# Columns 2 to 5 of an output projection by seven half-size products a pair instead of eight

## The chip, the cores and the metric

One core of one Trainium2 chip runs one launch of one decoder layer over 512 tokens of width 1024. The metric is the device time of the launch in microseconds, the median of several runs.

## The reference, cut to what matters

```python
h = x + 0.5 * swiglu(rmsnorm(x, g1), w1_in, w1_out)            # first feed-forward
h = h + hybrid_mixer(rmsnorm(h, gm), ...)                      # the mixer
h = h + 0.5 * swiglu(rmsnorm(h, g2), w2_in, w2_out)            # second feed-forward
y = rmsnorm(h, final)

def hybrid_mixer(u, ...):
    ...
    y = sigmoid(gate_h) * y_h + sigmoid(gate_g) * y_g          # (512, 1024), two merged branches
    return y @ w_out                                           # (1024, 1024): the output projection
```

The change is in the last line, `y @ w_out`, and in the adding of its result to `h`.

## The kernel before, in words

Activations lie transposed: a tile of 128 partitions (channels) by 512 tokens for each of eight channel blocks. A product in fp32 accuracy is three matmuls of float32r operands: both factors are split into a high part (a cast on ACT) and a low part (a subtraction on DVE), and `mm3` (lines 199 to 202) adds high x high, high x low and low x high in PSUM.

The layer has three stages: the first feed-forward, the mixer, the second feed-forward. Within the feed-forwards, and in nearly all of the mixer, the order of the work is fixed by hand or by a planner (`Desk`, which plays engines and tile rings in Python and issues instructions in that order). The mixer's output projection (lines 2250 to 2254) stands outside of both: there the framework's own scheduler orders the instructions, by priority and by its own estimate of durations, and moves them in front of one another.

What matters here, in the order of the program:

- `merged(d)` (line 1900) makes operand d of the output projection: it loads the branch and gate tiles (SP), combines them on DVE (lines 1917, 1920, 1923), and splits the result into `ms[d]`, high part by ACT (line 1930) and low part by DVE (line 1932). The eighth one comes last, after the last branch product.
- The output projection is a loop over eight output columns d. For each, SP loads the residual `hd[d]`, which the first feed-forward had spilled, and the two halves of the weight column (line 193, 256 KB each, into a ring `raw` of RB = 3 tiles); `slab` splits each half (ACT cast, line 195; DVE subtraction, line 196) into a ring `wp` of WB = 6 pairs (two tags of three); `dense` runs 8 x 3 matmuls of 512 columns; DVE adds half of the PSUM to the residual (line 2254) into `h[:, d]`.
- `nextnorm` (line 692) then prepares the second feed-forward for column d: `uh`, `ul` (ACT line 226, DVE line 227), a square (ACT, line 236), and its addition to `acc` on POOL (line 238). For d = 7 the addition is on DVE (line 697).
- The second feed-forward begins with plain units of four blocks each (12 matmuls of 512 columns). Its weights first come through the same `raw` and `wp` rings (line 311; casts on line 344, subtractions on line 319). After the first unit, PE runs the statistics matmul `pst` (line 247), which reads `acc`; matmuls behind it wait for it, since an engine runs its instructions in order. The loads into the feed-forward's own ring `rw` wait until the mixer's memory is free, which is after line 697.
- The feed-forwards already use seven products for eight in their large parts (`seven`, `fast`): there, an operand's low part is now and then made by an ACT negation (line 348) and an accumulating transfer on POOL that adds the weight from DRAM (line 349).

## Time and profile before

| | |
|---|---|
| device time, median of 3 runs | 1548.21 us (1547.71 to 1548.64) |
| the profiled execution's own time | 1547.87 us |
| its span in the trace | 1546.1 us |
| PE busy | 1535.9 us, 99% |
| DVE / ACT / POOL busy | 1179.7 / 887.9 / 409.0 us |
| granted TensorE clock, mean | 0.999 |

The profiled execution took 1.8 us beyond its span and 0.34 us less than the median. A busy PE means that matmuls are in its pipeline; how fast they follow one another is read from the distance of their starts. All times below are microseconds from the start of the span.

### The profile page before, as it was taken

The numbers are of one execution on the slowest core, as the hardware profiler recorded it, in microseconds if no ns is written. First come the engines' busy times: TensorE is split into PE (matmuls) and PEld (weight loads), VectorE is DVE, ScalarE is ACT, GpSimd is POOL, SyncE is SP. The second block draws the span as 40 slices with busy tenths as digits, with TensorE's granted clock in tenths as the row PEclk, the third lists the DMA queues.
The fourth block names the chain that finished last, engine by engine and source line by source line (L and its number), as shares of the span: only waits on it lengthen the run. The fifth ranks groups of instructions, "written<-read, shape, count | busy, mean of one in ns | idle before, by whom it ended". The sixth has DMA issues, their size and how long they took to land.

```text
span 1546.1 us, 29433 instructions
## 1 busy us (share of the span) xinstructions
PE 1535.9 (99%) x10660; PEld 1340.0 (87%) x10660; DVE 1179.7 (76%) x2257; ACT 887.9 (57%) x1965; POOL 409.0 (26%) x727
## 2 busy tenths in 40 slices
PE   9999999999999999999999999999999999999998
PEld 8899998988888888888888878888888899999897
DVE  6988887678786778678888887865554799988765
ACT  5766776454454345556676676555423576676543
POOL 0211221110221212536534655450001221121000
PEclk9999999999999999999999999999999999999999
DMA  5866866543213223654463675566554587786751
GB/s 190 190 167 171 190 163 150 154 120 109 84 45 94 65 81 117 191 181 147 134 208 119 190 224 164 171 191 187 153 192 130 157 185 194 194 194 172 192 123 64
DMA packets 159538, 237.57 MB, mean 154 GB/s; under 512 B 23312, under 2 KB 54672, under 8 KB 159392
## 3 DMA queue, kind: packets, MB, share of 16 engines
q1 hardware_dynamic: 138944, 199.63, 41.5%
q0 software_dynamic: 17568, 31.47, 12.7%
q10 hardware_dynamic: 2880, 4.59, 1.0%
q8 instruction: 84, 1.38, 0.4%
q14 instruction: 62, 0.51, 0.1%
HBM read 206.50 MB, written 29.13 MB: 152 GB/s over the span
## 4 chain that ended last, share of the span: by engine, by line
PE 96%; DMA 1%; ACT 1%; DVE 1%; issue 0%; SPq 0%; POOLq 0%; POOL 0%; ACTq 0%; DVEq 0%
PE pmm L200 17%; PE pmm L202 17%; PE pmm L201 17%; PE px L202 8%; PE px L200 8%; PE px L201 8%; PE pnat L200 4%; PE pnat L202 4%; PE pnat L201 4%; DMA kt<-kn 1%; PE pog L1738 1%; PE pgq L1530 1%; PE pw L1722 1%; PE pl L1277 1%; PE pd L1220 1%; PE pog L1736 1%
## 5 line engine op out<-in xcount | busy, mean ns | idle before, releaser
L200 PE MATMUL pmm<-uh,wp 128*128 128x512 f32 x863 | 355.2, 412 | 0.5 <-ACT ci L1397 0.3
L202 PE MATMUL pmm<-uh,wp 128*128 128x512 f32 x863 | 337.5, 391 | 0.0
L201 PE MATMUL pmm<-ul,wp 128*128 128x512 f32 x863 | 336.9, 390 | 0.0
L202 PE MATMUL px<-xs,wp 128*128 128x256 f32 x900 | 248.4, 276 | 0.0
L200 PE MATMUL px<-xs,wp 128*128 128x256 f32 x900 | 248.4, 276 | 0.0
L201 PE MATMUL px<-xs,wp 128*128 128x256 f32 x900 | 248.4, 276 | 0.0
L2103 DVE TENSOR_TENSOR wp<-raw,wp 128x512 fp32r<-128x512 f32 x226 | 159.3, 711 | 86.7 <-ACT wp L2101 83.5
L2101 ACT CAST wp<-raw 128x512 fp32r<-128x512 f32 x226 | 139.3, 619 | 137.0 <-PE pmm L202 106.5
L202 PEld LDWEIGHTS pmm<-uh,wp 128*128 128x128 f32 x863 | 162.0, 188 | 35.4
L200 PEld LDWEIGHTS pmm<-uh,wp 128*128 128x128 f32 x863 | 162.3, 188 | 33.2 <-ACT ci L1397 0.7
L201 PEld LDWEIGHTS pmm<-ul,wp 128*128 128x128 f32 x863 | 162.5, 188 | 29.7 <-DVE ul L1802 0.4
L200 PEld LDWEIGHTS px<-xs,wp 128*128 128x128 f32 x900 | 169.0, 188 | 0.1
L201 PEld LDWEIGHTS px<-xs,wp 128*128 128x128 f32 x900 | 168.9, 188 | 0.1
L202 PEld LDWEIGHTS px<-xs,wp 128*128 128x128 f32 x900 | 168.9, 188 | 0.0
L344 ACT CAST wp<-sw 128x512 fp32r<-128x512 f32 x176 | 107.9, 614 | 69.0 <-PE px L202 20.9
L319 DVE TENSOR_TENSOR wp<-sw,wp 128x512 fp32r<-128x512 f32 x176 | 120.8, 686 | 32.6 <-ACT wp L344 32.5
L344 ACT CAST wp<-rw 128x512 fp32r<-128x512 f32 (+1 forms) x132 | 80.7, 613 | 29.1 <-PE pnat L202 10.5
L1581 POOL TENSOR_TENSOR fm<-gfs,gln 128x60 f32<-128x60 f32 (+24 forms) x155 | 61.7, 398 | 92.8 <-DMA od<-zo 26.6
L1407 DVE SCALAR_TENSOR_TENSOR cy<-ci,cs,cy 128x512 f32<-128x512 f32 x96 | 72.2, 753 | 1.4
L1582 POOL TENSOR_TENSOR gln<-gln,fm 128x60 f32<-128x60 f32 (+24 forms) x155 | 64.4, 415 | 12.1
L349 POOL DMA_DIRECT2D wp<-w1b x40 | 34.7, 866 | 112.0 <-ACT wp L348 56.1
L378 DVE TENSOR_TENSOR sw<-rw 128x512 f32<-128x512 f32 x88 | 60.4, 686 | 1.7 <-DMA rw<-w2a 1.7
(587 smaller groups left out, 3496.4 us busy)
## 6 DMA issues: line engine op xcount, KB each, us to landing
raw<-wt SPq DMA_DIRECT2D x160, 256.0 KB
rw<-w1b SPq DMA_DIRECT2D x80, 256.0 KB
rw<-w1a SPq DMA_DIRECT2D x74, 256.0 KB
wp<-w1b POOLq DMA_DIRECT2D x40, 256.0 KB, 5.4
wp<-w1a POOLq DMA_DIRECT2D x35, 256.0 KB, 5.3
rw<-w2b SPq DMA_DIRECT2D x34, 256.0 KB
raw<-wn SPq DMA_DIRECT2D x32, 256.0 KB
raw<-wbg SPq DMA_DIRECT2D x32, 256.0 KB
```

Of the source, the lines that this page charges most:

```text
L200: pe.matmul(pt, ah, bh, start=first, stop=False)
L201: pe.matmul(pt, ah, bl, start=False, stop=False)
L202: pe.matmul(pt, al, bh, start=False, stop=last)
L319: dve.tensor_tensor(lo, x, hi.bitcast(F32), op=ALU.subtract)
L344: act.copy(hi, x)
L349: pool.dma_start(lo, units[i].fold, accum_op=ALU.add)
L378: dve.tensor_tensor(v[n], a, b, op=op)
L1407: dve.scalar_tensor_tensor(y, ci[:, j:j + T], wc[j], y, op0=ALU.mult, op1=ALU.add)
L1581: pool.tensor_tensor(tv, bc(m[:, j + 1:, j], w), t[:, j:j + 1, :w].to_broadcast([P, n, w]), op=ALU.mult)
L1582: pool.tensor_tensor(t[:, j + 1:, :w], t[:, j + 1:, :w], tv, op=ALU.add)
L2101: act.copy(hi, raw)
L2103: dve.tensor_tensor(lo, raw, hi.bitcast(F32), op=ALU.subtract)
```

## The change

Output columns 0, 1, 6 and 7 are computed as before. Columns (2, 3) and (4, 5) are computed as two pairs by Strassen's scheme in Winograd's form, over blocks: the weights' two columns and two halves of the 1024 inputs, and the tokens' two halves of 256. Seven products of 4 x 3 matmuls of 256 columns replace eight.

- `pieces(j)`, j = 0 to 3, forms the crossed operands from blocks j and j + 4 of the merged activations: four subtractions of 256 columns in place in `h`, then two high parts (ACT) and two low parts (DVE). For j < 3 the planner has them behind `merged(4 + j)`; j = 3 stands outside the planner. So that the blocks survive, `merged` writes its sum into `h[:, d]`, not into its own tile.
- `sevens(j)` computes a pair: SP loads four weight blocks `wr` (256 KB each, ring `vb` of 4), DVE makes four combinations `ws`, and `product` splits seven operands into `wp`. Two of the seven low parts (products 3 and 6) are made by an ACT negation and an accumulating transfer on POOL. DVE and ACT join the products out of PSUM (into `wv`, `wu`); the residual is added into `wv` by two accumulating transfers on POOL, no longer loaded by SP; the last sums go to `h`.

```diff
--- before.py
+++ after.py
@@ -49,6 +49,7 @@
 STAY = (15,)
 CONVS = 7
 SLACK = 0.8
+OUT = 0, 1, (2, 3), (4, 5), 6, 7
 TAIL = 3
 TURN = 22
 FRESH = 5
@@ -1897,6 +1898,80 @@
             return ab[:, 0], ab[:, 1]
         return make
 
+    def pieces(j):
+        x, y, lo, hi = h[:, j], h[:, 4 + j], slice(0, 256), slice(256, 512)
+        if j == 0:
+            homes = [t[:, i] for t in (places["gz"]("wz", (P, 2, T), F32R) for _ in range(2)) for i in range(2)]
+        elif j < 3:
+            homes = [places[n]("wq", dt=F32R) for n in (("on", "on", "qm", "ln"), ("gb", "gb", "at", "at"))[j - 1]]
+        else:
+            homes = [z[:, 6 + i] for i in range(2) for z in (uh, ul)]
+        crossed[j] = homes[:2], homes[2:]
+        less = lambda o, a, b: (V(256), lambda: dve.tensor_tensor(o, a, b, op=ALU.subtract))
+        yield less(x[:, lo], x[:, hi], x[:, lo])
+        yield less(x[:, hi], y[:, hi], x[:, hi])
+        yield less(y[:, hi], y[:, hi], x[:, lo])
+        yield less(y[:, lo], y[:, lo], y[:, hi])
+        for z, (a, b) in zip((x, y), crossed[j]):
+            yield A(512), lambda z=z, a=a: act.copy(a, z)
+            yield V(512), lambda z=z, a=a, b=b: dve.tensor_tensor(b, z, a.bitcast(F32), op=ALU.subtract)
+
+    def sevens(j):
+
+        def fetch(n, q):
+            r = places["vb"]("wr")
+            sp.dma_start(r, wo[2 * j + n][:, q * T:q * T + T])
+            return r
+        lo, hi = slice(0, 256), slice(256, 512)
+        moving = {0: lambda i: (ms[i], lo), 3: lambda i: (ms[4 + i], lo), 5: lambda i: (ms[4 + i], hi),
+                  1: lambda i: (crossed[i][0], lo), 4: lambda i: (crossed[i][0], hi),
+                  6: lambda i: (crossed[i][1], lo), 2: lambda i: (crossed[i][1], hi)}
+        a11, a21, a22, a12 = (fetch(*x) for x in ((0, 0), (1, 0), (1, 1), (0, 1)))
+        bank = [ps("px", x) for x in "abde"]
+        where = {3: (0, lo), 5: (0, hi), 6: (1, lo), 0: (2, lo), 2: (2, hi), 1: (3, lo), 4: (3, hi)}
+
+        def comb(x, y, f):
+            z = places["kn"]("ws")
+            with tc.high_priority():
+                dve.tensor_tensor(z, x, y, op=f)
+            return z
+
+        def product(o, x, src=None):
+            wl, wh = e["pair"](off=SHIFT)
+            with tc.high_priority():
+                act.copy(wh, x)
+                if src is None:
+                    dve.tensor_tensor(wl, x, wh.bitcast(F32), op=ALU.subtract)
+                else:
+                    act.mul(wl, wh.bitcast(F32), -1.0)
+                    pool.dma_start(wl, src, accum_op=ALU.add)
+            b, c = where[o]
+            for i in range(4):
+                k, (m, t) = slice(i * P, i * P + P), moving[o](i)
+                mm3(bank[b][:, c], wh[:, k], wl[:, k], m[0][:, t], m[1][:, t], i == 0, i == 3)
+        product(0, a11)
+        s1 = comb(a21, a22, ALU.add)
+        s2 = comb(s1, a11, ALU.subtract)
+        product(2, s2)
+        w = places["n2"]("wv", (P, 4 * 256))
+        u = places["x"]("wu", (P, 256))
+        act.mul(w[:, :256], bank[2][:, lo], 0.5)
+        dve.scalar_tensor_tensor(u, bank[2][:, hi], 0.5, w[:, :256], op0=ALU.mult, op1=ALU.add)
+        product(3, a12, wo[2 * j][:, T:])
+        product(1, s1)
+        product(4, comb(a11, a21, ALU.subtract))
+        uu, b4, u4 = (y.rearrange("p (a t) -> p a t", t=256) for y in (w[:, 256:768], bank[3], u))
+        dve.scalar_tensor_tensor(uu, b4, 0.5, u4.to_broadcast([P, 2, 256]), op0=ALU.mult, op1=ALU.add)
+        dve.scalar_tensor_tensor(w[:, 768:], bank[3][:, lo], 0.5, w[:, 512:768], op0=ALU.mult, op1=ALU.add)
+        for n in range(2):
+            pool.dma_start(w[:, n * T:n * T + T], hd[2 * j + n], accum_op=ALU.add)
+        product(6, a22, wo[2 * j + 1][:, T:])
+        product(5, comb(a12, s2, ALU.subtract))
+        act.copy(h[:, 2 * j + 1, hi], w[:, 768:])
+        for n, c in ((1, lo), (0, slice(0, T))):
+            dve.scalar_tensor_tensor(h[:, 2 * j + n, c], bank[n][:, c], 0.5, w[:, n * T:n * T + c.stop], op0=ALU.mult, op1=ALU.add)
+        return 2 * j, 2 * j + 1
+
     def merged(d):
 
         yield "on", ("K", 7) if d < 2 else "projected", ("y", d), ("t", d), ("t", 8 + d), *([("ms", d - 3)] if d > 2 else [])
@@ -1917,11 +1992,14 @@
         dve.scalar_tensor_tensor(mi, tg, 1.0, mi, op0=ALU.add, op1=ALU.mult)
         yield "on", ("wbg", d)
         yield *V(512), 1
-        dve.scalar_tensor_tensor(g, g, 1.0, pts[d], op0=ALU.add, op1=ALU.mult)
+        gt = g
+        dve.scalar_tensor_tensor(gt, gt, 1.0, pts[d], op0=ALU.add, op1=ALU.mult)
         D.put("a" if d in (2, 3) else "mm")
         yield V(512)
-        dve.tensor_tensor(g, g, mi, op=ALU.add)
+        g = h[:, d]
+        dve.tensor_tensor(g, gt, mi, op=ALU.add)
         D.put("mi")
+        D.put("ta")
         if dbg is not None and "m" in dbg:
             sp.dma_start(dbg["m"][:, d], g)
         yield A(512)
@@ -1930,8 +2008,11 @@
         act.copy(a, g)
         yield V(512)
         dve.tensor_tensor(b, g, a.bitcast(F32), op=ALU.subtract)
-        D.put("ta")
         D.fire(("ms", d))
+        if 4 <= d < 7:
+            for need, f in pieces(d - 4):
+                yield need
+                f()
 
     def closing():
 
@@ -1955,7 +2036,7 @@
 
     o_h = [None] * HH
     so, ms, pts = [None] * VH, [None] * 8, {}
-    stay = dict.fromkeys(STAY)
+    stay, crossed = dict.fromkeys(STAY), {}
     wbgs = [(d, q) for q in range(3) for d in (0, 1)] + [(d, q) for d in (2, 3) for q in range(3)] + [(d, 3) for d in range(4)] + \
         [(d, q) for d in range(4, 8) for q in range(4)]
     G = {"kq": [hv[:, i].rearrange("p (c a b) -> p c a b", c=NT, a=2) for i in range(3)]}
@@ -2247,12 +2328,19 @@
             sp.dma_start(dbg["og"][:, i], od[i])
 
 
-    for d in range(8):
+    for need, f in pieces(3):
+        f()
+    after = e["nextnorm"](C_F2, tag="ta", bufs=TA)
+    for step in OUT:
+        if isinstance(step, tuple):
+            for d in sevens(step[0] // 2):
+                after(d, mp)
+            continue
         hr = ta("hr")
-        sp.dma_start(hr, hd[d])
-        pt = dense(wo[d], KD, lambda k: ms[k])
-        dve.scalar_tensor_tensor(h[:, d], pt, 0.5, hr, op0=ALU.mult, op1=ALU.add)
-        e["nextnorm"](C_F2, tag="ta", bufs=TA)(d, mp)
+        sp.dma_start(hr, hd[step])
+        pt = dense(wo[step], KD, lambda k: ms[k])
+        dve.scalar_tensor_tensor(h[:, step], pt, 0.5, hr, op0=ALU.mult, op1=ALU.add)
+        after(step, mp)
```

How the instructions move, in three places.

SP's queue behind the last branch weights. `wr` are the weight blocks of the pairs, `raw` from `wo` those of the other columns, `raw` and `rw` from `w1b` the second feed-forward's, `hr` a residual. Before:

```order
L2066 DMA raw<-wbg 128x512 x3
L193 DMA raw<-wo 128x512 x12
L2252 DMA hr<-hd 128x512
L193 DMA raw<-wo 128x512 x2
L2252 DMA hr<-hd 128x512
L193 DMA raw<-wo 128x512 x2
L2252 DMA hr<-hd 128x512
L311 DMA raw<-w1b 128x512 x2
L2252 DMA hr<-hd 128x512
```

Now:

```order
L1923 DMA wr<-wo 128x512 x2
L2147 DMA raw<-wbg 128x512 x2
L1923 DMA wr<-wo 128x512
L2147 DMA raw<-wbg 128x512
L1923 DMA wr<-wo 128x512
L194 DMA raw<-wo 128x512 x7
L1923 DMA wr<-wo 128x512 x4
L194 DMA raw<-wo 128x512
L312 DMA raw<-w1b 128x512 x5
L2340 DMA hr<-hd 128x512 x2
L312 DMA raw<-w1b 128x512
```

The residuals of columns 6 and 7 (the last `hr`) now stand behind five loads of the second feed-forward.

DVE in front of the statistics matmul (`acc` is the last row of each; `ws` and `wp` from `wr` are weights of a pair, `wv` its joined products). Before:

```order
L2254 SCALAR_TENSOR_TENSOR h<-pmm,hr 128x512
L196 TENSOR_TENSOR wp<-raw,wp 128x512
L227 SCALAR_TENSOR_TENSOR ul<-h,cs,uh 128x512
L2254 SCALAR_TENSOR_TENSOR h<-pmm,hr 128x512
L319 TENSOR_TENSOR wp<-raw,wp 128x512 x2
L227 SCALAR_TENSOR_TENSOR ul<-h,cs,uh 128x512
L2254 SCALAR_TENSOR_TENSOR h<-pmm,hr 128x512
L319 TENSOR_TENSOR wp<-raw,wp 128x512 x2
L227 SCALAR_TENSOR_TENSOR ul<-h,cs,uh 128x512
L2254 SCALAR_TENSOR_TENSOR h<-pmm,hr 128x512
L319 TENSOR_TENSOR wp<-raw,wp 128x512 x2
L697 TENSOR_TENSOR acc<-acc,sqt 128x512
```

Now:

```order
L197 TENSOR_TENSOR wp<-raw,wp 128x512
L1965 SCALAR_TENSOR_TENSOR wv<-px,wv 128x256
L320 TENSOR_TENSOR wp<-raw,wp 128x512 x2
L1972 SCALAR_TENSOR_TENSOR h<-px,wv 128x512
L1972 SCALAR_TENSOR_TENSOR h<-px,wv 128x256
L228 SCALAR_TENSOR_TENSOR ul<-h,cs,uh 128x512 x2
L2342 SCALAR_TENSOR_TENSOR h<-pmm,hr 128x512
L320 TENSOR_TENSOR wp<-raw,wp 128x512 x2
L228 SCALAR_TENSOR_TENSOR ul<-h,cs,uh 128x512
L2342 SCALAR_TENSOR_TENSOR h<-pmm,hr 128x512
L320 TENSOR_TENSOR wp<-raw,wp 128x512 x2
L698 TENSOR_TENSOR acc<-acc,sqt 128x512
```

The second pair's joins and last sums, which wait for PSUM and for the accumulating transfers of `hd`, stand between the subtractions of the second feed-forward's first weights.

POOL from the mixer's last norm to the first low part of the second feed-forward. Before:

```order
L1765 TENSOR_TENSOR sm<-sm,mhalf 128x8 x2
L238 TENSOR_TENSOR acc<-acc,sqt 128x512 x6
L262 TENSOR_TENSOR rcol<-rcol,mhalf 128x4
L349 DMA wp<-w1b 128x512 x5
L349 DMA ws<-w1b 128x512
```

Now:

```order
L1766 TENSOR_TENSOR sm<-sm,mhalf 128x8 x2
L1947 DMA wp<-wo 128x512 x2
L239 TENSOR_TENSOR acc<-acc,sqt 128x512
L1947 DMA wp<-wo 128x512
L1967 DMA wv<-hd 128x512 x2
L1947 DMA wp<-wo 128x512
L239 TENSOR_TENSOR acc<-acc,sqt 128x512 x2
L1967 DMA wv<-hd 128x512 x2
L239 TENSOR_TENSOR acc<-acc,sqt 128x512 x3
L263 TENSOR_TENSOR rcol<-rcol,mhalf 128x4
L350 DMA wp<-w1b 128x512 x5
```

Four low parts of weights and four residuals are now issued by POOL, between the additions to `acc`.

## Rows read from the trace of the kernel before

**Rows 1.** The page: busy time of the engines; the chain that ended last, by engine.

```profile
PE 1535.9 (99%) x10660; PEld 1340.0 (87%) x10660; DVE 1179.7 (76%) x2257; ACT 887.9 (57%) x1965; POOL 409.0 (26%) x727
...
PE 96%; DMA 1%; ACT 1%; DVE 1%; issue 0%; SPq 0%; POOLq 0%; POOL 0%; ACTq 0%; DVEq 0%
```

**Rows 2.** Windows: columns us, then busy and count of PE, PEld, DVE, ACT, POOL, PEclk, DMA.

```profile
1180.00:1190.00 10.00, 10.00 (x46) 8.29 (x45) 5.53 (x8) 4.36 (x7) 1.84 (x2) 1.00 0.45 141
...
1260.00:1270.00 10.00, 10.00 (x91) 10.00 (x90) 9.25 (x15) 7.53 (x14) 2.60 (x3) 1.00 0.89 217
```

**Rows 3.** Timeline of PE: start us, us, engine, line, operation, tiles, shapes.

```profile
1165.38 0.39 PE L200 MATMUL pmm<-m,wp 128*128 128x512 f32 x1
...
1170.14 0.39 PE L200 MATMUL pmm<-m,wp 128*128 128x512 f32 x1
...
1244.10 0.28 PE L201 MATMUL px<-xs,wp 128*128 128x256 f32 x1
...
1247.28 0.28 PE L202 MATMUL px<-xs,ws 128*128 128x256 f32 x1
```

**Rows 4.** Timeline 1198 to 1214: SP, then ACT, DVE and PE, around the first statistics matmul.

```profile
1199.64 0.93 SPq L311 DMA_DIRECT2D raw<-w1b  x2
...
1200.62 0.42 SPq L2252 DMA_DIRECT2D hr<-hd  x1
...
1205.19 0.33 SPq L311 DMA_DIRECT2D raw<-w1b  x1
...
1209.14 1.14 ACT L344 CAST wp<-raw 128x512 fp32r<-128x512 f32 x2 [3.03 <-PE pmm L202]
...
1210.19 0.63 ACT L236 ACTIVATE sqt<-h 128x512 f32<-128x512 f32 x1
...
1209.80 1.29 DVE L319 TENSOR_TENSOR wp<-raw,wp 128x512 fp32r<-128x512 f32 x2
...
1211.01 0.68 DVE L697 TENSOR_TENSOR acc<-acc,sqt 128x512 f32<-128x512 f32 x1
...
1211.75 1.05 PE L247 MATMUL pst<-ones,acc 128*128 128x1 f32 x8
```

**Rows 5.** Waits in 1170 to 1216: us in total, times, longest.

```profile
PEld pst L247 <- DVE acc L697: 0.4, 1, 0.4
```

**Rows 6.** Groups of instructions in 1170 to 1212, DVE and ACT: count, busy, mean ns.

```profile
L196 DVE TENSOR_TENSOR wp<-raw,wp 128x512 fp32r<-128x512 f32 x9 | 6.1, 691 | 3.5 <-ACT wp L195 3.5
...
L227 DVE SCALAR_TENSOR_TENSOR ul<-h,cs,uh 128x512 fp32r<-128x512 f32 x8 | 6.0, 749 | 0.4
...
L226 ACT ACTIVATE uh<-h,cs 128x512 fp32r<-128x512 f32 x8 | 5.8, 721 | 0.3
...
L195 ACT CAST wp<-raw 128x512 fp32r<-128x512 f32 x9 | 5.6, 623 | 13.6 <-PE pmm L202 11.4 <-ACT sqt L236 1.6 <-ACT acc L233 0.6
```

**Rows 7.** Line 349, accumulating transfers: issue ns; to landing, whole run, then 1452 to 1470.

```profile
L349 POOL DMA_DIRECT2D wp<-w1b x40: 856/865/924, 1220.5 to 1410.5; - x40
...
DMA to landing us min/median/max: 3.7/5.1/7.5
...
DMA to landing us min/median/max: 4.1/4.3/4.5
```

**Rows 8.** Two SP issues, then windows of the transfers' bytes (last columns: DMA share, GB/s).

```profile
1194.19 0.33 SPq L311 DMA_DIRECT2D raw<-w1b  x1
...
1194.58 0.42 SPq L2252 DMA_DIRECT2D hr<-hd  x1
...
1195.20:1197.30 2.10, 2.10 (x11) 1.75 (x10) 0.00 (x0) 0.00 (x0) 0.99 (x1) 1.00 0.78 247
...
1200.60:1204.50 3.90, 3.90 (x19) 3.24 (x18) 0.99 (x3) 0.68 (x2) 1.33 (x1) 1.00 0.65 210
...
1206.00:1207.50 1.50, 1.50 (x8) 1.27 (x7) 0.43 (x1) 0.11 (x1) 1.25 (x1) 1.00 0.56 175
```

**Rows 9.** Windows: the end of the span, where PE runs nothing.

```profile
1543.00:1546.00 3.00, 0.00 (x0) 0.00 (x0) 0.00 (x0) 0.09 (x1) 0.00 (x0) 0.57 0.56 195
```

## The prediction

> **What bounds the kernel now.** I read the page first: PE is busy for 99% of the span, and 96% of the chain that ended last is PE [rows 1]. So only what shortens PE's stream, or makes it wait, moves the time. Then the windows of the stage: in ten microseconds of output projection PE has no idle time, while DVE is busy for 5.5, ACT for 4.4, POOL for 1.8 and the DMA for less than half [rows 2]. There is room beside PE for more preparation. The same view in the second feed-forward shows seven-product work: 91 matmuls instead of 46 in ten microseconds, with DVE at 9.3 and ACT at 7.5. Then PE's timeline for the pitch of a matmul [rows 3]: 21 matmuls of 512 columns start between 1165.38 and 1170.14, 0.2267 us each; 28 of 256 columns between 1244.10 and 1247.28, 0.1136 us each.
>
> Last, the end of the stage [rows 4]. PE's first unit of the second feed-forward is followed by the statistics matmul, which needs all eight squares in `acc`. The addition starts at 1211.01, takes 0.68, and the matmul starts at 1211.75. The list of waits has 0.4 us there [rows 5]. So in the kernel before, the end of DVE's and ACT's work and the end of PE's work arrive together. This is the point to watch: if PE gets shorter and the other chain doesn't, the matmul waits and the gain is gone.
>
> **PE's part.** A pair was 48 matmuls of 512 columns, 10.88 us; it becomes 84 of 256, 9.54 us by the pitch of rows 3. Two pairs: 2.7 us less. More matmuls cost nothing extra by these rows, since half the columns take half the time. The Trainium skill (TensorE: Matmul & The Clock Gate, Back-to-back issue gap) speaks against the change here: it gives each isolated matmul a fixed 2.5 ns beyond its columns; 72 more matmuls would cost 0.2 us and the saving would be 2.5, an estimate from that page. The rows show no such share. I take 2.7.
>
> **The preparation up to the first product.** Sixteen subtractions of 256 columns, eight casts and eight subtractions of 512 columns are added for the crossed operands, at 0.62 us a cast and 0.69 a subtraction [rows 6] at most: 16 us of DVE, 5 of ACT. Three of the four groups stand before column 0 begins at 1165.4, spread over some 40 us; with DVE about as loaded there as in rows 2, half of that time is free. The last group (blocks 3 and 7) needs the last merged operand; cast, subtractions and their turn in the queue put its end at about 1172, and product 2, its first reader, starts at 1177.6. Hidden. If that cover went, each microsecond of DVE would be one of PE.
>
> **The chain through the pairs.** An operand pair in `wp` becomes free six operands later, so a weight can be split only that far ahead. Slabs lasted 2.72 us on PE; a product lasts 1.36. The time ahead is halved, while a low part by transfer needs cast, negation, issue and landing. Landing takes 3.7 to 7.5 us, 5.1 in the median of the run, most of them in crowded stretches; two in a calm one took 4.1 and 4.5 [rows 7]. I take 4.3 and keep 3.7 and 5.1 as ends. For loads by SP the bytes tell: one alone, issued at 1205.19 [rows 4], is through by 1207.5; two, issued at 1194.19 and 1194.58, by 1197.3; three, from 1199.64 on, by 1204.5 [rows 4, 8]. So I take 2.4, 3.1 and 4.8 us; ends are 2.3 and 4.9 for any of them.
>
> With these I follow the chain in the changed order, in the clock of the trace before. Back to back, two casts take 1.14 us and two subtractions 1.29 [rows 4], so one costs 0.53 or 0.61 where another follows.
> 1. Column 1 ends at 1176.65 (from 1170.14 on, two matmuls of 256 columns that now slip in and 27 of 512, and 0.16 for the last one's end) and frees an operand pair; the cast for product 6 of pair one (0.62) frees a landing tile; SP loads the second pair's block: 2.7, until 1180.0.
> 2. DVE: two combinations and a preparation between them, 2.0, until 1182.0. ACT: two casts and a negation, 1.8, until 1183.9.
> 3. POOL: 0.3 to the issue, 0.9 for product 3's low part, then the first residual at 1185.1. The low part lands at 1188.4; PE wants it at 1188.7. The residual lands 4.3 later, 1189.4.
> 4. DVE adds column 2 (0.7); ACT prepares it, squares, copies, casts the first slab of column 6 (0.6, 0.5, 0.3, 0.6): 1192.3. Behind that a copy, column 3's preparation and square, and the casts of the next two slabs: 2.5, until 1194.8; the subtraction: 1195.6.
> 5. The tile so freed takes the second feed-forward's second load: 3.1, until 1198.8. Two casts and the subtractions behind them: 2.0, until 1200.8.
> 6. SP issues two more loads, and only then the residual of column 6, at 1201.2; in a group of four it lands after 4.8, at 1206.0. In the kernel before, this residual was never waited for.
> 7. DVE adds column 6 and makes a low part: 1.4, until 1207.4. That frees the tile of the sixth load: 2.4, until 1209.9, much as the load of 1205.19 did before. Two casts and the last square, 1.7, until 1211.6; the addition to `acc`, 0.7 and two steps between engines of 0.1: 1212.5.
>
> Preparations (0.75 on DVE, 0.72 on ACT, rows 6) are in these sums with 0.67 and 0.63 back to back.
>
> **The sum.** Before, 192 matmuls of the stage and 12 of the first unit, from 1165.38 on, end at 1211.6; PE alone would now be there 2.7 us earlier, at 1208.9. It waits until 1212.5, against 1211.75 before. Behind it everything is as before, and PE has no idle time there to give back. So: -2.7 for PE, +3.6 of wait, less the 0.1 that it waited already: **+0.8 us**. The profiled execution of 1547.87 becomes 1548.7; the median of the runs shown lies 0.34 higher, which gives **1549.0 us**. POOL's additions to `acc` cost nothing: by these steps the last of them ends 2 us before the last square.
>
> The ends: the chain cannot give more than PE's 2.7, so 1545.5 is the floor. With accumulating transfers at 5.1 the sum is 1.6, by the same steps; with SP landings half a microsecond longer each, it grows by 2. Both: about 1552.
>
> By the Trainium skill (DMA: Bandwidth & Descriptors, Anatomy of one DMA) a POOL transfer takes 2.0 us plus its bytes at 436 GB/s, for 256 KB an estimate of 2.6. The residual would then land 1.7 us earlier and the sum would be -0.9. Rows 7 have no transfer below 3.7, so I don't go by it.
>
> **The rivals.** A measurement of this kernel can tell about 0.2%, 3.1 us, from no change.
> - *The wait in front of the statistics matmul takes back the gain*, as summed: -1.5 to +3.1, 0.45.
> - *The cover holds.* Loads land some 0.4 us faster each, the chain ends by 1210 and PE keeps 1.5 to 2.7: 1545.5 to 1546.7. For it: DMA share under a half in the stage [rows 2]. Against it: seven steps in series with little slack in any. 0.25, and 0.05 of that for a measured gain over 0.2%.
> - *Slower, by the residuals behind SP's queue.* Places: the ring of three `raw` tiles and the last `hr` loads. Four SP landings lie in series (steps 1, 5, 6, 7), and each is in a group. If each takes 0.6 us more than I took, the sum is +3.2: 1551.4; at 0.9 more, 1552.6. From 0.6 on it decides. For it: three together took twice what one took [rows 8]. 0.18.
> - *The clock falls during the wait.* At the end of the span, where PE runs nothing, the granted clock is 0.57 on average over three microseconds, so part of them at the lower level [rows 9]; everywhere in the stage it is 1.00 [rows 2]. If a wait of 3.6 us did the same, twelve matmuls at half speed would cost 2.7 more: +3.5, 1551.7. The Trainium skill (TensorE: Matmul & The Clock Gate, Why this matters for your kernels) warns of idle gaps between bursts of matmuls; the rows show the fall only after the last matmul. 0.07.
> - *The change does less than it says.* The order lists 168 matmuls of 256 columns for 96 of 512, all in this stage; 0.05 for a stall that I don't see, either way.
>
> **How the numbers follow.** The likeliest is 1549.0. Faster by over 0.2% needs more than PE's whole gain: 0.05. Slower by over 0.2%: the third and fourth case, 0.25. The rest, 0.70, is within. From the floor of 1545.5 to 1552.5 I leave out less than 2 in 10.
>
> **What would show it.** Right: the stretch from column 0 to the first unit of the second feed-forward is 2.7 us shorter on PE, PE then stands idle for 2 to 5 us until `acc` is done, DVE waits before the sums of columns 4 and 6, and the matmuls behind are as before. Wrong: no idle time in front of the statistics matmul (then 1545.5); a wait of PE on an accumulating transfer inside the pairs; a granted clock below 1.00 behind the wait; or a pitch of more than 0.114 us in the pairs.

## The result and the profile after

The changed kernel takes **1557.89 us** (median of 4 runs, 1556.31 to 1559.04) against 1547.96 (4 runs, 1546.5 to 1548.64) on the same chip: a ratio of 1.0063, 95% interval 1.0051 to 1.0076. That is 9.9 us slower, where I forecast 0.8. Its profiled execution took 1558.24, with a span of 1556.5.

PE, never idle in the stage before [rows 2], now waits twice. The list of PE's waits from 1160 to 1235 (us in total, times, longest):

```profile
PE pst L248 <- DVE acc L698: 4.4, 1, 4.4
PE px L203 <- DMA wp<-wo: 2.0, 1, 2.0
```

The 4.4 us at the statistics matmul are the wait that I forecast. The 2.0 us come earlier, inside pair two, on an accumulating transfer. Behind both the clock is lower, which the windows show (columns as in [rows 2]):

```profile
1190.00:1200.00 10.00, 8.02 (x57) 7.66 (x56) 6.14 (x9) 4.60 (x10) 3.14 (x3) 0.87 0.57 103
1200.00:1210.00 10.00, 10.00 (x48) 8.44 (x47) 4.82 (x10) 2.97 (x6) 1.73 (x2) 0.96 0.85 230
1210.00:1220.00 10.00, 5.57 (x26) 4.41 (x24) 8.99 (x11) 5.93 (x11) 4.33 (x3) 0.89 0.12 32
1220.00:1230.00 10.00, 10.00 (x42) 8.44 (x43) 4.21 (x8) 3.51 (x6) 1.95 (x2) 0.77 0.92 308
```

PE's timeline says what it costs: behind the wait inside pair two matmuls of 256 columns start 0.21 us apart instead of 0.1136 [rows 3], behind the one at the statistics matmul those of 512 columns 0.43 instead of 0.2267, the lower of the clock's two levels:

```profile
1194.59 0.28 PE L202 MATMUL px<-wz,wp 128*128 128x256 f32 x1
1196.84 0.39 PE L203 MATMUL px<-wz,wp 128*128 128x256 f32 x1 [1.98 <-DMA wp<-wo]
...
1197.70 0.41 PE L202 MATMUL px<-wq,wp 128*128 128x256 f32 x1
1197.91 0.41 PE L203 MATMUL px<-wq,wp 128*128 128x256 f32 x1
...
1201.06 0.39 PE L201 MATMUL pmm<-m,wp 128*128 128x512 f32 x1
...
1214.48 0.39 PE L203 MATMUL pmm<-uh,wp 128*128 128x512 f32 x1
1219.30 1.86 PE L248 MATMUL pst<-ones,acc 128*128 128x1 f32 x8 [4.43 <-DVE acc L698]
...
1222.02 0.63 PE L203 MATMUL pmm<-uh,wp 128*128 128x512 f32 x1
1222.45 0.63 PE L201 MATMUL pmm<-uh,wp 128*128 128x512 f32 x1
```

What is late is on POOL's queue. Its timeline has four accumulating transfers within 3 us (low part of pair two's product 3, pair one's two residuals, low part of pair two's product 6), and pair two's residuals later:

```profile
1186.23 0.87 POOL L1947 DMA_DIRECT2D wp<-wo  x1 [3.33 <-PE px L203]
1187.09 1.79 POOL L1967 DMA_DIRECT2D wv<-hd  x2
1189.18 0.86 POOL L1947 DMA_DIRECT2D wp<-wo  x1 [0.31 <-ACT wp L1946]
...
1201.53 1.79 POOL L1967 DMA_DIRECT2D wv<-hd  x2 [2.05 <-DVE wv L1964]
```

By line, the low parts (L1947) and the residuals (L1967) land so:

```profile
L1947 POOL DMA_DIRECT2D wp<-wo x4: 857/870/924, 1171.9 to 1189.2; - x4
...
DMA to landing us min/median/max: 4.1/4.8/7.6
...
L1967 POOL DMA_DIRECT2D wv<-hd x4: 857/865/907, 1187.1 to 1202.5; - x4
...
DMA to landing us min/median/max: 6.0/6.2/6.5
```

The 7.6 is product 6's low part, issued last at 1189.18: PE starts on it at 1196.84. The residuals keep DVE from its sums, as its timeline shows (columns 2, 4 and 6, the last square, and the first scaling of the second feed-forward):

```profile
1193.36 0.69 DVE L1972 SCALAR_TENSOR_TENSOR h<-px,wv 128x512 f32<-128x512 f32 x1 [4.44 <-PE px L203]
...
1207.54 0.69 DVE L1972 SCALAR_TENSOR_TENSOR h<-px,wv 128x512 f32<-128x512 f32 x1 [2.17 <-DMA wv<-hd]
...
1212.15 0.68 DVE L2342 SCALAR_TENSOR_TENSOR h<-pmm,hr 128x512 f32<-128x512 f32 x1
...
1218.56 0.68 DVE L698 TENSOR_TENSOR acc<-acc,sqt 128x512 f32<-128x512 f32 x1
...
1227.24 2.74 DVE L468 SCALAR_TENSOR_TENSOR rooma<-h,cs,rbc 128x512 f32<-128x512 f32 x4 [2.46 <-ACT rbc L256]
```

At 1193.36 the releaser named is PE, but PE's part had ended some 6 us before: the 4.44 us were spent on the residual issued at 1187.09.

That late residual holds up pair two as well, on ACT and DVE, not on PE. ACT stands idle until column 2's sum, and the first join of pair two, whose product PE had finished by 1189, is behind that on ACT, at 1196.05. DVE's join at 1200.55 then stands behind subtractions for the weights of columns 6 and 7 that ran beside POOL's additions to `acc`: one took 1.17 us and two 2.37, where in the trace before one takes 0.69 and two 1.29 [rows 4, 6]. So pair two's residuals are issued at 1201.53 only. ACT, DVE and POOL:

```profile
1194.09 0.72 ACT L227 ACTIVATE uh<-h,cs 128x512 fp32r<-128x512 f32 x1 [4.51 <-DVE h L1972]
...
1196.05 0.37 ACT L1958 ACTIVATE wv<-px 128x256 f32<-128x256 f32 x1
...
1196.17 1.17 DVE L197 TENSOR_TENSOR wp<-raw,wp 128x512 fp32r<-128x512 f32 x1 [0.51 <-ACT wp L196]
...
1198.26 2.37 DVE L197 TENSOR_TENSOR wp<-raw,wp 128x512 fp32r<-128x512 f32 x2
1200.55 0.68 DVE L1964 SCALAR_TENSOR_TENSOR wv<-px,wu 128x512 f32<-128x512 f32 x1
...
1195.48 1.32 POOL L239 TENSOR_TENSOR acc<-acc,sqt 128x512 f32<-128x512 f32 x1 [5.44 <-ACT sqt L237]
1197.70 1.78 POOL L239 TENSOR_TENSOR acc<-acc,sqt 128x512 f32<-128x512 f32 x1 [0.90 <-ACT sqt L237]
```

To compare kernels I use three starts: PE's first matmul of the stage (S), the statistics matmul (Q) and that first scaling (R). Before: 1165.38, 1211.75, 1217.22. After: 1166.95, 1219.30, 1227.24. So 1.57 us were lost ahead of the stage, 5.98 between S and Q, 2.47 between Q and R: together 10.02, and nothing is given back later (the spans differ by 10.4). S after, and R before:

```profile
1166.95 0.39 PE L201 MATMUL pmm<-m,wp 128*128 128x512 f32 x1
...
1217.22 2.74 DVE L467 SCALAR_TENSOR_TENSOR rooma<-h,cs,rbc 128x512 f32<-128x512 f32 x4
```

### The profile page after: what moved, and what is told of

Same layout as the page of the kernel before. It is cut to its first block, busy times and chain, and to the rows that moved or that the text cites. A ratio compares the mean times of both kernels' runs of the same rounds, so it can differ in the third digit from the quotient of the medians.

```text
span 1556.5 us, 29654 instructions
## 1 busy us (share of the span) xinstructions
PE 1539.2 (99%) x10732; PEld 1345.7 (86%) x10732; DVE 1203.2 (77%) x2297; ACT 898.0 (58%) x1987; POOL 415.8 (27%) x735
## 4 chain that ended last, share of the span: by engine, by line
PE 93%; DMA 3%; DVE 2%; ACT 1%; issue 1%; SPq 0%; POOLq 0%; POOL 0%; ACTq 0%; DVEq 0%
PE pmm L201 16%; PE pmm L203 15%; PE pmm L202 15%; PE px L203 8%; PE px L201 8%; PE px L202 8%; PE pnat L201 4%; PE pnat L202 4%; PE pnat L203 4%; DMA kt<-kn 1%; PE pgq L1531 1%; PE pog L1739 1%; PE pw L1723 1%; PE pl L1278 1%; PE pd L1221 1%
## 5 line engine op out<-in xcount | busy, mean ns | idle before, releaser
L2184 DVE TENSOR_TENSOR wp<-raw,wp 128x512 fp32r<-128x512 f32 x226 | 159.5, 712 | 84.5 <-ACT wp L2182 81.4
```

What stands on the lines that cost most here:

```text
L2184: dve.tensor_tensor(lo, raw, hi.bitcast(F32), op=ALU.subtract)
```

## The experiments

The theories. **A**: accumulating transfers are dear, and in flight together hold each other up; that delays product 6's low part and the sums. **B**: SP's queue, with the residuals of columns 6 and 7 among weight loads, sets the end. **C**: the wait itself and the slow clock behind it are the price. **D**: the 1.57 us ahead of the stage are chance of the run.

| kernel | median, us | ratio to before, 95% interval | S | S to Q | Q to R | PE's waits in the stage, us |
|---|---|---|---|---|---|---|
| before | 1547.96 | | 1165.38 | 46.37 | 5.47 | 0.4 |
| the change | 1557.89 | 1.0063 [1.0051, 1.0076] | 1166.95 | 52.35 | 7.94 | 2.0; 4.4 |
| 1 residuals by SP and DVE | 1548.06 | 1.0001 [0.9991, 1.0010] | 1166.45 | 45.64 | 7.05 | 1.5 |
| 2 low parts by DVE | 1556.81 | 1.0053 [1.0038, 1.0068] | 1166.46 | 51.08 | 7.60 | 7.3 |
| 3 both | 1550.83 | 1.0019 [1.0009, 1.0028] | 1165.45 | 46.99 | 7.05 | 3.2 |
| 4 statistics one unit later | 1557.18 | 1.0057 [1.0042, 1.0072] | 1166.06 | 53.57 | 8.20 | 1.4; 4.1 |
| 5 residuals of 6, 7 early | 1556.45 | 1.0056 [1.0041, 1.0071] | 1163.83 | 51.51 | 7.60 | 0.7; 6.5 |
| 6 crossed operands alone | 1547.33 | 1.0000 [0.9991, 1.0010] | 1164.59 | 46.37 | 5.47 | 0.4 |
| 7 plain residuals by POOL | 1546.90 | 0.9996 [0.9987, 1.0006] | 1164.44 | 45.43 | 5.44 | 1.2; 0.2 |
| 8 filler matmuls | 1556.15 | 1.0053 [1.0038, 1.0068] | 1164.32 | 51.48 | 7.05 | 1.4; 2.5 |
| 9 price of transfers | 1548.24 | one run | 1165.68 | 46.37 | 5.45 | 0.4 |
| 10 one pair | 1546.67 | 0.9992 [0.9983, 1.0001] | 1166.09 | 44.96 | 5.39 | 0 |
| 11 as 7, product 6 by DVE | 1548.34 | 1.0001 [0.9992, 1.0010] | 1165.46 | 45.41 | 5.49 | 1.4 |
| 12 as 11, residuals early | 1547.51 | 0.9999 [0.9990, 1.0008] | 1165.37 | 45.26 | 5.47 | 0.2; 1.0 |
| 13 pairs before column 1 | 1552.54 | 1.0029 [1.0018, 1.0040] | 1164.61 | 51.09 | 5.45 | 0.5; 2.0; 0.8; 0.4 |
| 14 as 13, plain residuals | 1546.84 | 0.9992 [0.9983, 1.0001] | 1166.98 | 43.75 | 5.45 | 0 |

Each ratio is to runs of the kernel before on that run's own chip (medians 1547.37 to 1548.16), so the medians in the table don't divide to it. The last four columns are from one traced execution each, and that is not always a middling one: those of 5 and 8 are the shortest of four (1553.98 and 1553.87 us), that of 1 is the second longest of ten (1549.94), that of 14 the second longest of eleven (1547.74).

### 1 and 2. Which of the accumulating transfers

1 (the loads stand at the pair's start):

```diff
-            pool.dma_start(w[:, n * T:n * T + T], hd[2 * j + n], accum_op=ALU.add)
+            dve.tensor_tensor(w[:, n * T:n * T + T], w[:, n * T:n * T + T], hr[n], op=ALU.add)
```

> The residuals of columns 2 to 5 are loaded by SP and added by DVE, instead of four accumulating transfers; the low parts of products 3 and 6 still come by accumulating transfers. Theory A (accumulating transfers in flight together hold each other up: 6.0 to 7.6 us where one alone took 4.1): the low part of product 6 of pair two lands within 5 us, PE's wait of 2.2 us inside pair two is gone and with it the slow stretch of the clock behind it (1.7 us); the sums of columns 2 to 5 come 2 to 5 us earlier, so the wait of 4.4 us before the statistics matmul is under 1.5 us. Time 1547 to 1550 us. Theory B (the order of SP's queue sets the end of the chain, the landing of the accumulating transfers only shows it): four more loads stand on SP, the wait before the statistics matmul stays at 3 us or more and the clock falls there: 1552 to 1556 us. Theory D (the first matmul of the stage stands 1.57 us later than before by chance of the run, not by the change): its start lies within 1 us of either of the two, with the same instructions ahead of it.

2:

```diff
-        product(3, a12, wo[2 * j][:, T:])
+        product(3, a12)
...
-        product(6, a22, wo[2 * j + 1][:, T:])
+        product(6, a22)
```

> The low parts of products 3 and 6 are made by DVE, as in products 5 and 7; the residuals still come by four accumulating transfers, now two at a time instead of four. Theory A: the wait of PE inside pair two (2.2 us) and the slow clock behind it (1.7 us) are gone; the residuals land in 4.3 to 5 us instead of 6.2, so the sums of columns 2 and 4 come 1 to 2 us earlier; some wait before the statistics matmul stays (2 to 4 us, of which PE's earlier arrival makes part): 1551 to 1554 us. Theory B: the wait inside the pairs goes too, but nothing else moves: PE arrives 3.9 us earlier at the statistics matmul and waits 8 us: 1557 to 1558 us.

Without the residuals' transfers all of the loss between S and Q is gone (45.64 us), though SP carries four loads more: A, against B. The wait that was left was 1.5 us, and the clock fell behind it too:

```profile
1212.00:1214.00 2.00, 1.92 (x11) 1.75 (x12) 0.86 (x3) 0.00 (x0) 0.58 (x1) 0.85 0.33 119
1214.00:1216.00 2.00, 2.00 (x6) 1.54 (x5) 0.00 (x0) 0.35 (x1) 0.45 (x1) 0.50 0.97 312
```

That is so in this execution. Four of the ten have a mean clock of 0.998, this one among them, and took 1548.66 to 1550.26 us; the other six have 0.999 and took 1546.78 to 1548.07.

In 2 I was wrong: I gave 1551 to 1554 by A, and it took 1556.81, nearer to what I gave by B (1557 to 1558, with 8 us of wait). So 2 taken alone does not speak for A; 1, 5 and 7 do. PE no longer waits inside the pairs, but the residuals, now two at a time, still land after 4.1, 5.6 and 6.3 us (least, median, most). Column 4's sum stands on DVE behind a subtraction that waited until 1205.05 for a load of the second feed-forward's weights, which was in flight together with the residuals. The squares come barely earlier, and PE, earlier itself, waits for them:

```profile
PE pst L248 <- DVE acc L698: 7.3, 1, 7.3
```

### 3. Both

The edits of 1 and 2 together.

> No accumulating transfer in the pairs: the residuals by SP and DVE, the low parts of products 3 and 6 by DVE. Theory A: as the variant with the residuals alone, or up to 1 us better: no wait of PE inside the pairs, under 1.5 us before the statistics matmul, granted clock 1.00 through the stage: 1546 to 1549 us. Theory B: the wait before the statistics matmul stays at 3 us or more: 1552 to 1556 us. A third way: DVE, with eight low parts and four sums more, becomes what PE waits for inside the pairs; then the trace names DVE as the releaser of weights in the pairs, and the time is 1552 us or more.

A's 1546 to 1549 was missed, at 1550.83. No accumulating transfer is left, the clock is 1.00 inside the pairs, but 3.2 us of wait stand before the statistics matmul; DVE is busy without a break from 1180 to 1200. The wait of over 3 us is what I gave as B's sign. But SP's loads are those of 1; what 3 adds to it is DVE's four subtractions, and with them S to Q is 1.35 us longer. So the third way came true in another place than I said: DVE delays the sums, not the weights.

### 4 and 8. The wait and the clock

4: in the plan of the second feed-forward the statistics stand one unit later. 8: 16 matmuls before them.

```diff
-                hooks[1], hooks[2] = ([f] for f in stats(fp, acc))
-                start = 3
+                hooks[2], hooks[3] = ([f] for f in stats(fp, acc))
+                start = 4
...
+            for _ in range(fill):
+                pe.matmul(pt, uh[:, 0, :P], uh[:, 1], start=True, stop=True)
```

> The change as it is, but the statistics matmuls of the second feed-forward stand one unit later (after its second unit), so that PE has a unit's 12 matmuls, 2.7 us, more work before it needs the squares. Theory C (the wait itself and the clock that falls behind it are the price: 4.4 us of wait, 2.4 us of slow clock): the wait shrinks to 1.7 us; if that is too short for the clock to fall, both 2.7 and 2.4 us come back: 1552.5 to 1553.5 us; if the clock falls all the same, 2.7 us alone: 1555 us. The wait inside pair two and its slow clock stay, 3.9 us. If the end of the squares moves later with it (the chain hangs on PE's units and not on the preparation), nothing comes back: 1557 to 1558 us.

> The change as it is, with 16 matmuls of 512 columns added to PE's stream in front of the statistics matmul of the second feed-forward; they write a bank that the statistics matmul then overwrites, and fill 3.6 us of the 4.4 us wait. Theory C (the clock falls because PE stands idle, and the eight matmuls of 0.427 instead of 0.227 us behind the wait, with the slow statistics matmuls, cost 2.4 us of themselves): the granted clock stays at 1.00 behind the wait, the matmuls behind it are back at 0.227 us, the wait ends at the same moment: 1555 to 1556 us, 2 to 2.6 us less than the change. If the slow stretch has another cause, it stays, and the time is 1557.5 to 1558.5 us.

4 gave back nothing. The next unit needs the same late columns as operands, so PE waited for those:

```profile
PE pmm L202 <- DVE ul L228: 2.2, 2, 1.7
PE pmm L201 <- ACT uh L227: 1.9, 1, 1.9
PE px L203 <- DMA wp<-wo: 1.4, 1, 1.4
```

8 is inconclusive on the clock. In this run PE came earlier than in the change, so 2.5 us of wait were left behind the filler, and the clock fell behind those; from Q to R it took 7.05 instead of 7.94. The late columns, not the place of the statistics, are the cause; the slow clock adds 1.6 to 2.5 us to a wait.

### 5. The residuals of columns 6 and 7

```diff
+    both = places["fs"]("hr", (P, 2, T))
+    early = {d: both[:, d - 6] for d in (6, 7)}
+    for d in early:
+        sp.dma_start(early[d], hd[d])
```

> The change as it is, but the residuals of columns 6 and 7 are loaded before the pairs, into a tile of their own, so that they no longer stand on SP between the loads of the second feed-forward's weights. Theory A (the accumulating residuals of columns 2 to 5 set the end of the chain): the sums of columns 4 and 5 stay where they are, at the landing of their residuals; the wait before the statistics matmul shrinks by at most 0.6 us: 1556.5 to 1558 us. Theory B (the residuals behind SP's queue set it): the wait of 4.4 us before the statistics matmul goes to under 2, and the slow clock behind it with it: 1551 to 1554 us.

From S to Q it took 51.51 us: B, as I had it among the rivals, is out as the cause. The wait at the statistics matmul did not shrink, as both theories had it: it grew to 6.5 us, since PE lost less inside the pairs (0.7 us, with the clock at 1.00) and came earlier.

### 6. The crossed operands alone

```diff
-OUT = 0, 1, (2, 3), (4, 5), 6, 7
+OUT = range(8)
```

> The crossed operands are prepared as in the change (16 subtractions of 256 columns, eight casts and eight subtractions of 512), but all eight columns are made by eight products as before; nothing reads the crossed operands. It prices the preparation alone. Theory D and my prediction (the preparation is hidden, and the 1.57 us by which the stage began later belongs to the run): no change, 1547 to 1549.5 us, PE without idle time in the stage and 0.4 us before the statistics matmul. If the preparation costs time: the first matmul of the stage or a later one waits for DVE, 1549.5 to 1551 us.

46.37 and 5.47 us, both equal to the kernel before. The preparation is hidden, as forecast. S lies between 1163.83 and 1166.98 over all these kernels; the mean of the fourteen with crossed operands is 1165.50, and the two without have 1165.38 and 1165.68 (9): D holds.

### 7 and 9. Accumulating, or POOL's queue

7 puts plain transfers where the accumulating ones stood; 9 adds transfers that nothing reads to the kernel before.

```diff
-            pool.dma_start(w[:, n * T:n * T + T], hd[2 * j + n], accum_op=ALU.add)
+            pool.dma_start(hr[n], hd[2 * j + n])
+        for n in range(2):
+            dve.tensor_tensor(w[:, n * T:n * T + T], w[:, n * T:n * T + T], hr[n], op=ALU.add)
```

> The residuals of columns 2 to 5 are loaded by POOL at the very place of the accumulating transfers, but as plain transfers into tiles of their own; DVE adds them. Theory A1 (accumulating is what is slow: about 2.1 us of all 16 DMA engines for each 256 KB, against some 0.7 us for a plain load): they land within 3 us of their issue, product 6's low part within 5 us, the wait inside the pairs is under 0.5 us, the sums of columns 2 and 4 come 2 to 3 us earlier less 0.7 of DVE: 1548 to 1551 us. Theory A2 (it is POOL's queue and the moment of the issue, not the accumulation): they land after 5 us or more, the sums come later by DVE's additions, 1556 to 1560 us.

> The kernel before, with transfers on POOL that nothing reads, during columns 1 to 5 of the output projection: one accumulating transfer of 256 KB alone, then four accumulating ones issued together, and later three plain ones together and two single plain ones, all into the same tiles. It prices the transfers without the rest of the change. Theory A1: the accumulating one alone lands in about 4.1 us, the four together one after the other, some 1.7 to 2.1 us apart, the last 9 us or more after its issue less the spacing of the issues (6 to 8 us); the plain ones land in 2 to 3.5 us, the three together within 4.5 us. Theory A2 (POOL's queue is slow for any transfer, or the 6.0 to 7.6 us came from the crowd of the pairs): accumulating and plain ones land alike. The time stays that of the kernel before, 1546 to 1550 us, since nothing waits for them.

7 is better than I expected (1548 to 1551), for a reason beside the price: a plain load does not read the half-made sum, so the scheduler issues it long before the joins. The residuals landed in 2.8 to 4.9 us, and the first sum of pair two's columns came 10 us after their issue. So 7 mixes price and earliness. What it still waits for inside the pairs is product 6's low part, which still accumulates:

```profile
PE px L203 <- DMA wp<-wo: 1.2, 1, 1.2
```

9 prices the transfers alone. In it the one that was to land alone was issued together with the four, so it has no landing of a single one, and the landings missed what I gave: plain ones took 3.7 us and more, not 2 to 3.5. Its shares of the 16 engines' time, by queue (q0 POOL's, q1 SP's), from 1180 to 1186 with accumulating transfers and from 1191 to 1195 with plain ones:

```profile
q0 software_dynamic: 434, 0.79, 84.5%
q1 hardware_dynamic: 158, 0.29, 18.4%
...
q1 hardware_dynamic: 432, 0.79, 54.9%
q0 software_dynamic: 192, 0.60, 36.9%
```

84.5% of 6 us for 0.79 MB, three transfers, is 1.7 us of all 16 engines for each; plain ones on the same queue take 36.9% of 4 us for 0.60 MB, 0.64 us for 0.26. Landing, by line, the accumulating ones first:

```profile
DMA to landing us min/median/max: 5.2/7.9/9.8
...
DMA to landing us min/median/max: 3.7/5.2/7.1
```

The changed kernel has the same price: from 1186 to 1197 only these four use the engines, and 61.6% of 11 us for four is again 1.7 us each.

```profile
q0 software_dynamic: 576, 1.05, 61.6%
```

So the price in A1 stands, with 1.7 us instead of the 2.1 that I gave: four in flight take the engines for 6.8 us together. The plain one of 9 that landed after 7.1 us, issued at 1184.33, was in flight with them; the last, issued at 1195.44, took 3.7. How much of the change's loss is this price, and how much is that an accumulating transfer has to wait for the joins, is not shown: no run issues plain transfers behind the joins. That the second counts is likely from 2, where pair one's first residual landed after 4.1 us and the loss stayed.

### 10. One pair

```diff
-OUT = 0, 1, (2, 3), (4, 5), 6, 7
+OUT = 0, 1, (2, 3), 4, 5, 6, 7
```

> Only columns 2 and 3 by seven products, with the accumulating transfers as in the change; columns 4 and 5 by eight as before. The residuals of pair one land as late as in the change, but four columns of 5.4 us on PE lie behind them. Theory A (it is the distance from the last accumulating residual to the statistics matmul that costs): no wait inside the pair over 0.5 us, at most 0.4 us before the statistics matmul, granted clock 1.00; PE saves half of 2.7 us: 1.3 us less than before, 1545.5 to 1547 us. If a pair costs by itself (4 us each): 1551 to 1553 us.

As expected: no wait, and 1.41 us less between S and Q, half of PE's 2.7. The residuals landed after 4.3 to 5.7 us, and four columns of PE hid it.

### 11 and 12. What is left without them

11: 7 with `product(6, a22)`. 12: 11 with the loads of 5.

> The residuals of columns 2 to 5 by plain transfers on POOL and additions on DVE, and the low part of product 6 by DVE; only product 3's low part accumulates. The variant with plain residuals alone had one wait left inside the pairs, 1.2 us for product 6's low part, and 0.2 us before the statistics matmul, whose last square followed the end of column 7 on PE. Theory A: the 1.2 us go, the end of column 7 and the last square come 1.2 us earlier with it: 1.7 us less than before, 1545.5 to 1546.5 us where the kernel before has 1547.4 to 1548. If DVE's two more subtractions or the loads then end last, 0.5 to 1.2 us come back before the statistics matmul, and the clock may fall: 1546.5 to 1548.5 us.

> As the variant with plain residuals and product 6's low part by DVE, and the residuals of columns 6 and 7 loaded before the pairs, so that SP has two loads less among the second feed-forward's weights. Theory B in what is left of it (SP's queue sets the end once the accumulating transfers are gone): 0.5 us or more less than that variant, if that one waits before the statistics matmul. Theory A alone: no difference over 0.3 us.

11 missed: the 1.2 us inside the pairs went, and 1.4 came up before the statistics matmul (the second branch of the expectation). ACT has two casts of the second feed-forward's weights ahead of the last square; they began at 1208.26, when the sixth load had landed, and the square ran at 1209.30:

```profile
1208.26 1.14 ACT L345 CAST wp<-raw 128x512 fp32r<-128x512 f32 x2 [2.11 <-DMA raw<-w1b]
1209.30 0.63 ACT L237 ACTIVATE sqt<-h 128x512 f32<-128x512 f32 x1
```

So in this trace the load is the second limit, with S to R 0.9 us shorter than before; the medians show no gain (1548.34 against 1548.03). 12 moves the trace by 0.15 us, less than the 0.3 to 0.5 that would decide.

### 13 and 14. Another order of the columns

```diff
-OUT = 0, 1, (2, 3), (4, 5), 6, 7
+OUT = 0, (2, 3), (4, 5), 1, 6, 7
```

> The change with another order of the columns: 0, then the pairs, then 1, 6 and 7. Same work, same accumulating transfers; a third column of 5.4 us on PE now lies between the pairs and the statistics matmul. Theory A with distance (the late residuals cost only because the statistics matmul stands too close behind them): the 4.4 us of wait there go to zero, and the clock stays at 1.00 there; the wait for product 6's low part inside a pair stays (0 to 2 us, with up to 1.7 us of slow clock): 1545.5 to 1549 us. If the preparation of the last crossed operands, which the pairs now meet 5.4 us sooner, is late: a wait of PE for DVE in the first pair, 1 to 3 us more. If the order makes no difference, the chain of late residuals moves along with the work behind it, and the time stays at 1556 to 1558 us.

> The same order of the columns, with the residuals of the pairs by plain transfers on POOL and additions on DVE. With the loads' chain given 5.4 us more and no landing over 5 us: PE keeps nearly its whole 2.7 us, less a wait of up to 1.2 us for product 6's low part: 1545 to 1546.5 us, and the first of all these variants to be surely faster than the kernel before. If the crossed operands are late for the first pair: 1546.5 to 1549 us, with a wait of PE for DVE there.

13 lies between its branches. The wait before the statistics matmul fell to 0.4 us, but the same late sums now hold up, on ACT and DVE, the casts of the second feed-forward's first weights and a sum of an output column. PE waits for these, with a slow clock behind:

```profile
PE pmm L201 <- ACT wp L345: 2.0, 1, 2.0
PE pmm L201 <- DVE h L2342: 0.8, 1, 0.8
```

So distance alone does not do it; that the transfers accumulate counts. 14 has neither wait nor slow clock:

```profile
1170.00:1180.00 10.00, 10.00 (x79) 9.56 (x78) 9.01 (x17) 6.82 (x13) 0.85 (x1) 1.00 0.47 134
1180.00:1190.00 10.00, 10.00 (x91) 10.00 (x90) 9.89 (x16) 7.53 (x15) 6.88 (x6) 1.00 0.59 133
...
1200.00:1210.00 10.00, 10.00 (x46) 8.29 (x45) 7.38 (x11) 4.99 (x10) 2.85 (x3) 1.00 0.31 105
```

43.75 and 5.45 us: 2.64 less than before from S to R, all that PE saves. By the clock of the whole run it is 1546.84 against 1548.16, an interval that still touches 1. It is the lowest of these kernels in the stage; that it beats the kernel before is likely, not shown.

## Why the prediction was wrong

- **PE's part** was right. One pair gives 1.4 us, two give 2.6 where nothing waits (10, 14), at the pitch of rows 3.
- **The preparation** was right: it costs nothing (6). (24 subtractions at 0.69 are 16.6 us of DVE, where I wrote 16.)
- **The mechanism** was right in kind: the chain to the last square ends behind PE's work, and PE waits at the statistics matmul. Its path was not, as the next two points say.
- **The term that failed** is step 3, the landing of an accumulating transfer at 4.3 us. I took it from two in a calm stretch, issued 4.1 us apart and so hardly in flight together, and kept 5.1 as the end. Measured: 4.1 for the first of the four (product 3's low part), 6.0 to 6.5 for the residuals, 7.6 for the last. What I overlooked is in the change itself: it issues four within 3 us, and they share the engines. The 7.5 in rows 7 was there, and I put it down to crowds that others make. For pair two's residuals it is such a crowd: from 1201.5 to 1208.5 SP's loads take 51.6% of the 16 engines and these two 46.3%.
- **The chain from there**, in the clock of the trace before (after less 1.57 us):

| step | forecast | measured |
|---|---|---|
| 3: first residual of pair one issued | 1185.1 | 1185.5 |
| 3, 4: its landing, sum of column 2 | 1189.4 | 1191.8 |
| 7: sum of column 6 | 1206.0 | 1210.6 |
| 7: last square added | 1212.5 | 1217.7 |

Step 3 alone is 2.4 us. Step 6 failed with it: I let the residual of column 6 behind SP's loads decide, and followed no residual of columns 4 and 5. In the run those decide. Pair two's joins stand on ACT and DVE behind pair one's late sum; then the residual lands 6 us after its issue at 1201.53, the sum of column 4 starts at 1207.54, and column 6 stands behind it on DVE, without the wait of DVE that I gave as a sign. Two accumulating landings lie in series where I had one. I also put POOL's additions at nothing: ahead of pair two's join they go with some 1.6 us of longer subtractions on DVE. That is read from the trace; no run takes them away.
- **The product 6 low part** was the wait that I named as a sign of being wrong. In step 3 I held product 3's low part against PE's need, and not that of product 6, issued behind it and the residuals. It cost 2.0 us and a slow stretch.
- **The clock** was a rival at 0.07, with 2.7 us for one wait. It came true behind both waits: 1.7 us (22 matmuls that take 4.2 us instead of 2.5) and 2.5 (Q to R). The Trainium skill (TensorE: Matmul & The Clock Gate, Why this matters for your kernels) warns of idle gaps between bursts of matmuls; the trace agrees for the 4.4 us, with 0.50 where before it was 1.00, and shows the same behind 2.0, a gap shorter than those it warns of. I let a place where the trace before shows no idle PE speak for a high clock.
- **The rivals**: "behind SP's queue" named the right sign and the wrong queue (5). "The cover holds" is what happens with plain transfers and one column more (14).
- **The Trainium skill's price** (DMA: Bandwidth & Descriptors, Anatomy of one DMA), an estimate of 2.6 us for 256 KB, is near the best plain transfer on POOL here, 2.8 (7); the medians are 3.1 (14) to 5.2 (9). For accumulating ones no run here shows less than 3.4 (8), so it was right not to use it, and wrong to think that 4.3 was safe.

The sum as measured, S to R: 2.7 less for PE, 2.1 and 4.5 more of wait (by the distance of the starts, less what stood there before), 1.7 and 2.5 of slow clock, 0.1 of a small wait for product 3's low part: 8.2, against 8.45 read from the traces. The other 0.2 I did not place. With the 1.57 of chance ahead of the stage it is the 10 us of the traced execution. That the medians differ by as much, 9.9, is in part luck: chance ahead of the stage should not show in them, and the other three executions have no trace.

## What to carry to other kernels

Price a transfer that accumulates by the engines' time it takes and by what else is in flight with it, not by the landing of one alone; a plain load with an addition on a free engine can also be issued before the partial sum exists. When PE gets shorter, follow every late operand to the next wait of PE, and add the slow clock behind a wait to its price. Put work with late results where the most independent work still lies ahead of their reader.

## What the runs showed of the hardware

- An accumulating transfer of 256 KB takes 1.7 us of all 16 engines, a plain one on the same queue 0.64 (9).
- The granted clock fell behind single waits of PE of 1.5 (1), 2.0 (the change) and 2.5 us (8), and stayed at 1.00 behind one of 1.2 (7) and two of 1.4 (8, 11), each after a long busy stretch. Behind the 2.0 us and in 1 it fell when PE was running again, and stayed at 0.50 for some 3 us; in the change's 4.4 us it was at 0.50 from 1218 on, before PE began, and until 1224. What decides it is not shown.
- Subtractions on DVE that ran beside one of POOL's additions took 1.17 us for one and 2.37 for two, instead of 0.69 and 1.29 (the change).
- Between S and R the kernel before took 51.84 us, and so did 6; 9 took 51.82. Where PE waits for nothing, a stage can be compared to some hundredths across traced executions whose totals differ by 1.1 us.
